# Row sums formed early, two groups in the seventh block, and the seventh split issued behind the third's, in a macaron FFN

## The chip, the cores and the metric

One core of a Trainium2 chip runs one launch of the whole layer. The time is the device time of that launch in microseconds (us), the median of several runs. The engines are TensorE (PE; its weight loads are PEld), VectorE (DVE), ScalarE (ACT), GpSimd (POOL) and SyncE (SP, which issues most transfers).

## The reference

One layer on x of 256 tokens by 2048 columns in float32:

```
x = x + 0.5 * swiglu(rms_norm(x, ffn1_norm), w_gate1, w_up1, w_down1)
h = rms_norm(x, mix_norm);  u, q, k, v = split(h @ w_in)
x = x + concat(rms_norm(s5_mixer(u)), rms_norm(stick_breaking(q, k, v))) @ w_out
x = x + 0.5 * swiglu(rms_norm(x, ffn2_norm), w_gate2, w_up2, w_down2)
x = x + rms_norm((p @ w_ple_proj) * sigmoid(rms_norm(x, ple_norm) @ w_ple_gate), ple_post_norm)

swiglu(h, w_gate, w_up, w_down) = (silu(h @ w_gate) * (h @ w_up)) @ w_down
```

D_MODEL is 2048 and D_FF 5632. The change concerns the two FFNs, above all gate and up of the first.

## The kernel before

**Tiles.** The 256 tokens are two halves t of 128 rows. The 5632 columns of gate and up are eleven blocks f of 512 columns (f = 0 to 10, the "first" to the "eleventh" block). The 2048 rows of a weight are 16 tiles of 128, taken in four quarters kb of four tiles: one load on SP's queue brings 128 x 4 x 512 floats (1 MB) into a `raw` tile, of which there are five buffers.

**Split numbers.** To get float32 accuracy from the fast matmul form each operand is the sum of a high and a low part. For a weight half (two of the four tiles, 128 x 1024) ACT casts the high part (`split`, L181: `whi` or `shi`) and DVE subtracts it from the original for the low part (L184: `wlo` or `slo`). Three products are formed, high x high, high x low of the activations, and low x high: in an ordinary half (`gemm_half`, L322, L323, L327) these are 12 matmuls of 128 x 128 x 512. `weight_pair` hands out the buffers from two rings that alternate, "whi"/"wlo" with four buffers and, in the blocks with seven products, "shi"/"slo" with three. So the letters w and s are buffers, not kinds of operands.

**Seven products for eight.** The class `Seven` (from L463) treats gate and up together. `column` is the ordinary way for one of the two matrices and some quarters. `chunk` (L505) does one quarter of both, a group, with seven products instead of eight. It loads two raw tiles, gate (halves b11, b21) and up (halves b12, b22); forms t1 = b11 + b12, t2 = t1 + b22 and t4 = t2 + b21 on DVE (L501); lets a transfer on POOL's queue add b22 into b12 in place (L525, an accumulating DMA); and issues the products in the order 1 (b11), 5 (t1), 6 (t2), 4 (t4), 2 (b21), 3 (b22), 7 (the b12 that the transfer has changed). Each product is one split and six matmuls (L494, L495, L497), 42 for a group where two ordinary quarters issue 48. On the side of the activations it needs sums of rows: `whole_rows` joins high and low (DVE, L443), `sum_forms` makes four sums (DVE, L458) and splits them (ACT, then DVE: `hhi`, `hlo`).

**The blocks.** In the first FFN the blocks f = 0 to 5 go the ordinary way, since the preparation of the S5 mixer (`s5_prep`, small DVE and ACT instructions, L765 and following) holds memory beside them; `early` is 6. At f = 6 the preparation is finished, its memory is given back, and the row sums of both groups are formed. This seventh block does one group, kb = 0, and takes the other three quarters of both matrices by `column`. The blocks f = 7 to 10 do two groups (kb = 0 and 1). In the second FFN all blocks use `Seven`, the first with one group. The down projections mix groups and columns by a plan.

**The order.** A scheduler gives each engine its order of instructions; the program's order is its starting point, and it may put an instruction ahead of earlier ones that aren't ready by its own reckoning. Each engine then works its queue strictly in order. `step()` advances work that stands beside the main loop, `put_off(n, fn)` calls fn after n such steps, and the positions of instructions can be tied with `pin` or with the scheduler's `issue_after`, under which what is issued in the block stands behind a given instruction. A pool opened with `phase` takes the memory that earlier pools have left, tile by tile.

Of the kernel before, what the change touches and what calls it, by code (L numbers as in the profile page):

```python
# [26 lines left out]
NB = 512  # L27
# [6 lines left out]
def layer_kernel(ctx: ExitStack, tc: tile.TileContext, a: dict, shapes: dict, out: bass.AP):  # L34
# [143 lines left out]
    def split(hi, lo, src, scale=None, pinned=False):  # L178

        if scale is None:  # L180
            copy = nc.scalar.copy(hi, src)  # L181
            if pinned:
                pin(copy)
            nc.vector.tensor_tensor(out=lo, in0=src, in1=hi.bitcast(F32), op=ALU.subtract)  # L184
        else:
            split_each(hi.unsqueeze(1), lo.unsqueeze(1), src.unsqueeze(1), [scale])
# [276 lines left out]
    class Seven:  # L463


        def __init__(self, act, sums, ws, pool):
            self.act, self.sums, self.ws, self.pool = act, sums, ws, pool
            self.banks = {}
            self.begun = set()
# [17 lines left out]
        def product(self, z, left, src, final):  # L487
            hi, lo = weight_pair()
            split(hi, lo, src)
            ps = self.bank(z)  # L490
# [13 lines left out]
        def chunk(self, kb, final=()):  # L504

            if ring[0] is None:
                ring[:] = [self.pool, 0]
            raws = []
# [12 lines left out]
            def summed(z):  # L521
                return [[u[:, z, j * P : (j + 1) * P] for j in range(2)] for u in sums]
# [11 lines left out]
            self.product(2, whole(1, 0), b21, final)  # L534
            self.product(3, summed(3), b22, final)
            step()
            self.product(7, summed(2), b12, final)
            step()
# [16 lines left out]
    def ffn(i, xn, nxt, bg=None):  # L555
# [3 lines left out]
        early = 6 if bg else 0  # L559
        sevens = None if bg else pools.enter_context(sums_phase(f"sums{i}"))  # L560
        hp = pools.enter_context(phase(f"h{i}"))
        side = ExitStack()
        prep = bg(side) if bg else None
        mids = {}

# [13 lines left out]
        for f in range(NF):  # L579
            if prep and f == early:  # L580
                finish(prep)
                side.close()
                prep = None
                sevens = pools.enter_context(sums_phase(f"sums{i}"))
                hp = pools.enter_context(phase(f"h{i}b"))
                sums = [sum_forms(sevens, whole_rows(sevens, xn(kb)), "h") for kb in range(2)]
            if sevens:
                sg, hh = com("sg"), com("h")
# [15 lines left out]

                s = Seven(xn, lambda kb: sums[kb], ((wg, f * NB), (wu, f * NB)), sevens)
                if f == 0:
                    sums = [sum_forms(sevens, whole_rows(sevens, xn(0)))]
                    s.column(0, (1,))
# [6 lines left out]
                    sums.append(sum_forms(sevens, whole_rows(sevens, xn(1))))  # L615
                elif f == early:
                    s.column(0, (1, 2, 3))
                    s.chunk(0, (*shared, 2, 4))
                    put_off(0, opened, s)
                else:  # L620
                    s.chunk(0)
                    s.column(0, (2, 3))
                    s.chunk(1, (*shared, 2, 4))
                    put_off(0, opened, s)
                put_off(0, gated, s)
                s.column(1, (3,) if f == 0 else (1, 2, 3) if f == early else (2, 3), True)
                nc.vector.tensor_tensor(out=hh, in0=s.banks[3.8], in1=hh, op=ALU.add)
# [4 lines left out]
                put_off(2, turned, hp, f, hh)  # L632
                continue

            def gate():
# [71 lines left out]
        for n in range(0, ND, 2):  # L707
# [6 lines left out]

            s = Seven(kept, summed, ((wd, n * NB), (wd, (n + 1) * NB)), sevens)
            plan = plans[n // 2]
# [965 lines left out]
```

## Time and profile before

| | us |
|---|---|
| median of three runs | 1828.03 |
| the three runs | 1827.74 to 1829.2 |
| the profiled execution, whole time | 1829.07 |
| its span, first to last instruction | 1827.3 |

The mean granted TensorE clock of the profiled execution is 0.998 of full speed. Weights make most of the 425 MB that are moved. A row of the timeline has the start in us from the span's begin, the duration in us, the engine, the line, the operation, what is written from what, the shape, how many instructions the row holds, and in brackets the idle time ahead of it and what ended that. A row of windows has the stretch, its length, the busy time of PE, PEld, DVE, ACT and POOL with their number of instructions, the granted clock, the share of the DMA engines and GB/s. A row of waits has the total, the number and the longest. Successive matmuls overlap in the records, so a rate is read from one start to the next.

### The profile page before, as it was taken

How to read it: one execution, taken by the hardware profiler on the slowest of the kernel's cores; microseconds unless marked ns; L12 is line 12 of the kernel's file. 1: busy time of each engine (PE TensorE's matmuls, PEld its weight loads, DVE VectorE, ACT ScalarE, POOL GpSimd, SP SyncE). 2: the span in 40 equal slices, each digit the busy share in tenths (PEclk: the TensorE clock that was granted, in tenths of full speed). 3: DMA queues.
4: the chain of work that ended last, by engine and by line, in shares of the span. 5: the costliest groups of instructions: out<-in, count | busy, mean ns of one | idle time of the engine just before them, and what ended most of it. 6: DMA issues, size and time to landing. Idle time of an engine off the chain costs nothing.

```text
span 1827.3 us, 24177 instructions
## 1 busy us (share of the span) xinstructions
PE 1817.7 (99%) x8954; PEld 1504.9 (82%) x8954; DVE 1518.4 (83%) x1773; ACT 1048.0 (57%) x1220; POOL 101.0 (6%) x156
## 2 busy tenths in 40 slices
PE   9999999999999999999999999999999999999998
PEld 7888888888888888888898888888878888888887
DVE  8966759999898885697567899999989999888565
ACT  7444445655565665456695566555555556556554
POOL 0010000000000001010021000000000010000000
PEclk9999999999999999999999999999999999999999
DMA  9899877787777677674646788887777787667563
GB/s 328 282 286 281 247 226 231 235 246 220 254 246 238 189 250 229 186 252 156 220 149 213 241 280 234 265 258 222 241 220 236 237 274 241 226 202 250 172 217 127
DMA packets 234407, 425.27 MB, mean 233 GB/s; under 512 B 24272, under 2 KB 48240, under 8 KB 234128
## 3 DMA queue, kind: packets, MB, share of 16 engines
q1 hardware_dynamic: 223872, 390.06, 64.9%
q0 software_dynamic: 9696, 32.25, 8.1%
q8 instruction: 70, 1.15, 0.3%
q10 hardware_dynamic: 720, 1.41, 0.2%
q14 instruction: 49, 0.40, 0.1%
HBM read 372.41 MB, written 10.88 MB: 210 GB/s over the span
## 4 chain that ended last, share of the span: by engine, by line
PE 98%; DMA 1%; DVE 0%; ACT 0%; issue 0%; SPq 0%; ACTq 0%; DVEq 0%
PE acc L322 18%; PE acc L323 18%; PE acc L327 18%; PE aux L323 7%; PE aux L327 7%; PE aux L322 7%; PE acc L497 4%; PE acc L495 4%; PE acc L494 4%; PE aux L497 3%; PE aux L495 3%; PE aux L494 3%; DMA raw<-raw 1%; PE aux L1142 0%; PE acc L1398 0%; PE acc L1393 0%
## 5 line engine op out<-in xcount | busy, mean ns | idle before, releaser
L184 DVE TENSOR_TENSOR wlo<-raw,whi 128x1024 fp32r<-128x1024 f32 x486 | 589.0, 1224 | 179.3 <-ACT whi L181 177.9
L181 ACT CAST whi<-raw 128x1024 fp32r<-128x1024 f32 x486 | 505.3, 1050 | 352.5 <-PE acc L323 234.7
L322 PE MATMUL acc<-whi,nhi 128*128 128x512 f32 x1052 | 412.4, 392 | 0.9 <-ACT whi L181 0.4
L323 PE MATMUL acc<-whi,nlo 128*128 128x512 f32 x1052 | 409.6, 389 | 0.0
L327 PE MATMUL acc<-wlo,nhi 128*128 128x512 f32 x1052 | 288.8, 389 | 0.0
L184 DVE TENSOR_TENSOR slo<-raw,shi 128x1024 fp32r<-128x1024 f32 x180 | 219.2, 1218 | 32.7 <-ACT shi L181 31.3
L322 PEld LDWEIGHTS acc<-whi,nhi 128*128 128x128 f32 x1052 | 197.6, 188 | 43.9 <-ACT whi L273 1.4
L181 ACT CAST shi<-raw 128x1024 fp32r<-128x1024 f32 x180 | 188.7, 1050 | 76.1 <-DMA raw<-in_ffn_w_down 22.8
L327 PEld LDWEIGHTS acc<-wlo,nhi 128*128 128x128 f32 x1052 | 197.5, 188 | 41.1
L323 PEld LDWEIGHTS acc<-whi,nlo 128*128 128x128 f32 x1052 | 197.6, 188 | 40.1
L181 ACT CAST whi<-sum 128x1024 fp32r<-128x1024 f32 x68 | 71.6, 1053 | 136.5 <-DVE sum L501 129.9
L181 ACT CAST shi<-sum 128x1024 fp32r<-128x1024 f32 x52 | 54.8, 1053 | 85.4 <-DVE sum L501 83.0
L501 DVE TENSOR_TENSOR sum<-sum,raw 128x1024 f32<-128x1024 f32 x80 | 97.6, 1220 | 0.7
L525 POOL DMA_DIRECT2D raw<-raw x40 | 34.7, 868 | 955.3 <-DVE sum L501 657.6
L184 DVE TENSOR_TENSOR wlo<-sum,whi 128x1024 fp32r<-128x1024 f32 x68 | 83.1, 1221 | 2.4 <-ACT whi L181 1.6
L184 DVE TENSOR_TENSOR slo<-sum,shi 128x1024 fp32r<-128x1024 f32 x52 | 63.5, 1221 | 2.4 <-ACT shi L181 1.9
L322 PE MATMUL aux<-whi,hhi 128*128 128x512 f32 x168 | 65.4, 389 | 0.0
L323 PE MATMUL aux<-whi,hlo 128*128 128x512 f32 x168 | 65.4, 389 | 0.0
L323 PE MATMUL acc<-whi,hlo 128*128 128x512 f32 x160 | 62.3, 390 | 0.0
L322 PE MATMUL acc<-whi,hhi 128*128 128x512 f32 x160 | 62.2, 389 | 0.0
L322 PE MATMUL aux<-whi,nhi 128*128 128x512 f32 x156 | 60.7, 389 | 0.0
L323 PE MATMUL aux<-whi,nlo 128*128 128x512 f32 x156 | 60.7, 389 | 0.0
(375 smaller groups left out, 3200.2 us busy)
## 6 DMA issues: line engine op xcount, KB each, us to landing
raw<-in_ffn_w_up SPq DMA_DIRECT2D x88, 1024.0 KB, 6.1
raw<-in_ffn_w_down SPq DMA_DIRECT2D x88, 1024.0 KB, 5.3
raw<-in_ffn_w_gate SPq DMA_DIRECT2D x86, 1024.0 KB, 8.0
raw<-in_w_in SPq DMA_DIRECT2D x32, 1024.0 KB, 5.8
raw<-raw POOLq DMA_DIRECT2D x40, 512.0 KB, 5.9
raw<-in_w_out SPq DMA_DIRECT2D x16, 1024.0 KB, 5.2
raw<-in_w_ple_gate SPq DMA_DIRECT2D x16, 1024.0 KB, 5.3
hT<-mid SPq DMA_DIRECT2D x160, 64.0 KB, 4.3
```

Of the source, the lines that this page charges most:

```text
L181: copy = nc.scalar.copy(hi, src)
L184: nc.vector.tensor_tensor(out=lo, in0=src, in1=hi.bitcast(F32), op=ALU.subtract)
L322: nc.tensor.matmul(ps[t], lhsT=lh, rhs=hi[:, j, cols], start=start and j == 0, stop=False)
L323: nc.tensor.matmul(ps[t], lhsT=ll, rhs=hi[:, j, cols], start=False, stop=False)
L327: nc.tensor.matmul(ps[t], lhsT=lh, rhs=lo[:, j, cols], start=False, stop=stop and j == 1)
L494: nc.tensor.matmul(ps, lhsT=lh[j], rhs=hi[:, j], start=begin and j == 0, stop=False)
L495: nc.tensor.matmul(ps, lhsT=ll[j], rhs=hi[:, j], start=False, stop=False)
L497: nc.tensor.matmul(ps, lhsT=lh[j], rhs=lo[:, j], start=False, stop=z in final and j == 1)
L501: nc.vector.tensor_tensor(out=t, in0=x, in1=y, op=ALU.add)
L525: nc.gpsimd.dma_start(b12, b22, accum_op=ALU.add)
```

## The change

`split` now returns its two instructions, and in every group of both FFNs, the down projections included, the split and the matmuls of product 7 are issued behind the cast and the subtraction of product 3. The row sums of the first FFN's two groups are no longer formed at the seventh block but put off from the start of the sixth (f = 5), by 8 and 12 steps. Their pool (`sevens`) opens at the start of the FFN; the "shi"/"slo" ring gets a pool of its own (`turns`) at the seventh block. That block takes the ordinary path of the blocks behind it: two groups, and the quarters 2 and 3 by `column`.

```diff
@@ split
-            nc.vector.tensor_tensor(out=lo, in0=src, in1=hi.bitcast(F32), op=ALU.subtract)
+            rest = nc.vector.tensor_tensor(out=lo, in0=src, in1=hi.bitcast(F32), op=ALU.subtract)
+            return copy.ins, rest.ins
@@ class Seven, product
-            split(hi, lo, src)
+            self.last = split(hi, lo, src)
@@ class Seven, chunk
             if ring[0] is None:
-                ring[:] = [self.pool, 0]
+                ring[:] = [self.turns, 0]
...
             self.product(3, summed(3), b22, final)
+            copied, rest = self.last
             step()
-            self.product(7, summed(2), b12, final)
+            with tc.issue_after(copied), tc.issue_after(rest):
+                self.product(7, summed(2), b12, final)
@@ ffn
         early = 6 if bg else 0
-        sevens = None if bg else pools.enter_context(sums_phase(f"sums{i}"))
+        sevens = pools.enter_context(sums_phase(f"sums{i}"))
...
+        turns = sevens
+        sums = []
...
                 side.close()
                 prep = None
-                sevens = pools.enter_context(sums_phase(f"sums{i}"))
+                turns = pools.enter_context(phase(f"turns{i}"))
                 hp = pools.enter_context(phase(f"h{i}b"))
-                sums = [sum_forms(sevens, whole_rows(sevens, xn(kb)), "h") for kb in range(2)]
-            if sevens:
+            if f >= early:
...
-                elif f == early:
-                    s.column(0, (1, 2, 3))
-                    s.chunk(0, (*shared, 2, 4))
-                    put_off(0, opened, s)
                 else:
                     s.chunk(0)
                     s.column(0, (2, 3))
                     s.chunk(1, (*shared, 2, 4))
                     put_off(0, opened, s)
                 put_off(0, gated, s)
-                s.column(1, (3,) if f == 0 else (1, 2, 3) if f == early else (2, 3), True)
+                s.column(1, (2, 3) if f else (3,), True)
...
+            if f == early - 1:
+                for kb in range(2):
+                    put_off(8 + 4 * kb, lambda kb: sums.append(sum_forms(sevens, whole_rows(sevens, xn(kb)), "h")), kb)
```

Lines behind these places stand one to four further down in the changed program (L184 stays, L443 becomes L444, L494 becomes L495).

First place: ACT's queue at the second group of the eighth block in the second FFN. A `raw` with the smaller number (11500, 11517) is gate, the one with the larger (11502, 11519) is up; `shi_11571` is the cast of the seventh product before, `whi_11561` that of the third, `whi_11541` that of the fourth.

```order
L181 CAST whi_11507<-raw_11500 128x1024
L181 CAST shi_11517<-sum_11504 128x1024
L181 CAST shi_11551<-raw_11500 128x1024
L181 CAST whi_11529<-sum_11527 128x1024
L181 CAST shi_11571<-raw_11502 128x1024
L181 CAST whi_11541<-sum_11539 128x1024
L181 CAST whi_11561<-raw_11502 128x1024
L181 CAST whi_11583<-raw_11581 128x1024
```

And in the changed program, where the seventh is `shi_11588`, the third `whi_11578` and the fourth `whi_11558`:

```order
L181 CAST whi_11524<-raw_11517 128x1024
L181 CAST shi_11534<-sum_11521 128x1024
L181 CAST shi_11568<-raw_11517 128x1024
L181 CAST whi_11546<-sum_11544 128x1024
L181 CAST whi_11558<-sum_11556 128x1024
L181 CAST whi_11578<-raw_11519 128x1024
L181 CAST shi_11588<-raw_11519 128x1024
L181 CAST whi_11600<-raw_11598 128x1024
```

The seventh's cast has moved behind the fourth's and the third's; the subtractions on DVE have moved in the same way. Of the 40 groups before, five have the seventh's cast ahead of the third's on ACT: that of the seventh block in the first FFN and four in the second FFN.

Second place: ACT's queue at the seventh block's group in the first FFN. Before, `whi_2708` is the seventh, `shi_2677` the fourth and `shi_2697` the third; the raw tiles 2718 belong to the column behind it.

```order
L181 CAST whi_2640<-raw_2633 128x1024
L181 CAST shi_2651<-sum_2637 128x1024
L181 CAST whi_2664<-sum_2662 128x1024
L181 CAST whi_2687<-raw_2633 128x1024
L181 CAST whi_2708<-raw_2635 128x1024
L181 CAST whi_2720<-raw_2718 128x1024
L181 CAST shi_2677<-sum_2675 128x1024
L181 CAST shi_2697<-raw_2635 128x1024
```

And in the changed program, at the first group of that block, with `shi_2573` the fourth, `shi_2595` the third and `whi_2609` the seventh:

```order
L181 CAST whi_2536<-raw_2529 128x1024
L181 CAST whi_2560<-sum_2558 128x1024
L181 CAST shi_2547<-sum_2533 128x1024
L181 CAST whi_2584<-raw_2529 128x1024
L181 CAST shi_2573<-sum_2571 128x1024
L181 CAST shi_2595<-raw_2531 128x1024
L181 CAST whi_2609<-raw_2531 128x1024
L181 CAST whi_2621<-raw_2619 128x1024
```

The seventh has moved from ahead of the fourth to behind the third, and the column's first cast behind all of them.

Third place: DVE's queue at the start of the program, in the first block's second quarter (`nlo` are the low parts of the activations). Before:

```order
L277 TENSOR_TENSOR wlo_147<-raw_132,whi_146 128x512
L193 SCALAR_TENSOR_TENSOR nlo_165<-h_138,gains,nhi_164 128x256 x4
L184 TENSOR_TENSOR wlo_201<-raw_133,whi_200 128x1024
L184 TENSOR_TENSOR wlo_205<-raw_133,whi_204 128x1024
L193 SCALAR_TENSOR_TENSOR nlo_223<-sg_220,gains,nhi_222 128x256 x4
```

And in the changed program:

```order
L278 TENSOR_TENSOR wlo_150<-raw_135,whi_149 128x512
L194 SCALAR_TENSOR_TENSOR nlo_168<-h_141,gains,nhi_167 128x256 x4
L444 TENSOR_TENSOR whole_2363<-nhi_145,nlo_146 128x1024
L184 TENSOR_TENSOR wlo_204<-raw_136,whi_203 128x1024
L184 TENSOR_TENSOR wlo_208<-raw_136,whi_207 128x1024
L194 SCALAR_TENSOR_TENSOR nlo_226<-sg_223,gains,nhi_225 128x256 x4
```

The first of the row sums' instructions (`whole`, the join of high and low) stands in the first block, ahead of the second quarter's first low half; the rest of both groups' row sums follow it in the same block, between the low halves and the instructions of the S5 preparation, which stand further back by that.

In all, TensorE issues six matmuls fewer, DVE six instructions more, ACT three more, and POOL one accumulating transfer more (41 instead of 40).

More of the change, by code (lines that the diff above doesn't have):

```diff
@@ L463, in layer_kernel, with __init__ @@
     class Seven:
-        def __init__(self, act, sums, ws, pool):
-            self.act, self.sums, self.ws, self.pool = act, sums, ws, pool
+        def __init__(self, act, sums, ws, pool, turns):
+            self.act, self.sums, self.ws, self.pool, self.turns = act, sums, ws, pool, turns
             self.banks = {}
@@ L603, in gated @@
                     )
-                s = Seven(xn, lambda kb: sums[kb], ((wg, f * NB), (wu, f * NB)), sevens)
+                s = Seven(xn, lambda kb: sums[kb], ((wg, f * NB), (wu, f * NB)), sevens, turns)
                 if f == 0:
-                    sums = [sum_forms(sevens, whole_rows(sevens, xn(0)))]
+                    sums.append(sum_forms(sevens, whole_rows(sevens, xn(0))))
                     s.column(0, (1,))
@@ L713, in end @@
                 put_off(0 if m == ND - 1 and m < nxt.early else 2, nxt.block, m)
-            s = Seven(kept, summed, ((wd, n * NB), (wd, (n + 1) * NB)), sevens)
+            s = Seven(kept, summed, ((wd, n * NB), (wd, (n + 1) * NB)), sevens, turns)
             plan = plans[n // 2]
```

## The prediction

> **What bounds the kernel now.** I read the page's first and fourth parts first, to see which engine sets the end.
>
> ```profile
> span 1827.3 us, 24177 instructions
> PE 1817.7 (99%) x8954; PEld 1504.9 (82%) x8954; DVE 1518.4 (83%) x1773; ACT 1048.0 (57%) x1220; POOL 101.0 (6%) x156
> PE 98%; DMA 1%; DVE 0%; ACT 0%; issue 0%; SPq 0%; ACTq 0%; DVEq 0%
> ```
>
> TensorE is busy 1817.7 of 1827.3 us and holds 98% of the chain that ended last. So only three things can move the time: the number of matmuls, the gaps between them, and the rate at which they run. How fast do they run undisturbed? The timeline of PE alone, in an easy stretch, has two heads of equal groups of six:
>
> ```profile
> 1328.70 0.39 PE L322 MATMUL acc<-whi,nhi 128*128 128x512 f32 x1
> 1330.06 0.39 PE L322 MATMUL acc<-whi,nhi 128*128 128x512 f32 x1
> ```
>
> 1330.06 - 1328.70 = 1.36 us for six, 0.227 each (the 0.39 of a row overlaps the next one). Next the waits of PE by what released them, which say where the gaps are:
>
> ```profile
> PE acc L494 <- ACT whi L181: 1.9, 1, 1.9
> PE acc L322 <- ACT whi L181: 0.4, 1, 0.4
> PE aux L497 <- DVE wlo L184: 0.4, 1, 0.4
> ```
>
> The columns are the total, the number of times and the longest. One wait, 1.9 us at L494, is most of it. The "DMA 1%" of the chain points at the same place, so I read the timeline and the chain there (the eighth block of the second FFN, its second group).
>
> ```profile
> 1333.96 9.53 DMA raw<-raw
> 1338.92 1.22 DVE L501 TENSOR_TENSOR sum<-sum,raw 128x1024 f32<-128x1024 f32 x1
> 1343.65 1.04 ACT L181 CAST shi<-raw 128x1024 fp32r<-128x1024 f32 x1 [6.97 <-DMA raw<-raw]
> 1344.60 1.04 ACT L181 CAST whi<-sum 128x1024 fp32r<-128x1024 f32 x1
> 1345.55 1.99 ACT L181 CAST whi<-raw 128x1024 fp32r<-128x1024 f32 x2
> 1344.73 1.23 DVE L184 TENSOR_TENSOR slo<-raw,shi 128x1024 fp32r<-128x1024 f32 x1 [4.59 <-ACT shi L181]
> 1345.87 1.22 DVE L184 TENSOR_TENSOR wlo<-sum,whi 128x1024 fp32r<-128x1024 f32 x1
> 1343.21 0.61 PE L497 MATMUL aux<-wlo,nhi 128*128 128x512 f32 x2
> 1345.70 0.50 PE L494 MATMUL acc<-whi,hhi 128*128 128x512 f32 x1 [1.87 <-ACT whi L181]
> 1347.14 1.22 PE L497 MATMUL acc<-wlo,hhi 128*128 128x512 f32 x2 [0.25 <-DVE wlo L184]
> 1350.65 0.39 PE L494 MATMUL aux<-whi,nhi 128*128 128x512 f32 x1
> 1345.60:1348.00 2.40, 2.06 (x6) 1.44 (x7) 2.40 (x3) 2.40 (x4) 0.00 (x0) 0.82 0.04 15
> 1348.00:1350.60 2.60, 2.60 (x7) 2.04 (x7) 2.60 (x4) 2.60 (x4) 0.00 (x0) 0.51 0.37 62
> ```
>
> This is a queue standing behind a transfer. The accumulating DMA, which makes the seventh product's weights in place (b12 += b22), takes 9.53 us and lands at 1343.49. ACT has the seventh's cast (1343.65) ahead of the fourth's (1344.60) and the third's, and idles 6.97 us, though the fourth's sum has been ready since 1338.92 + 1.22 = 1340.14. PE, whose order is 4, 2, 3, 7, waits for the fourth's cast. The last two rows are windows; the eighth column, behind POOL's, is the granted TensorE clock: it falls to 0.82 and then 0.51, so the wait is paid twice.
>
> What is lost there: product 6's last matmul begins one pitch behind 1343.21, at 1343.44, so the fourth would begin at 1343.67 and the third two products later, at 1343.67 + 2 x 1.36 = 1346.39. It begins at 1350.65: **4.26 us lost**, 2.03 of it the late begin (1345.70 - 1343.67), the other 2.23 in twelve matmuls that take 4.95 instead of 2.72, mostly the half clock.
>
> [...]
>
> **The change part by part.**
>
> *Seven behind three.* The two forced positions hold ACT's cast and DVE's low half of product 7 until those of product 3 are issued. In the order of the changed program this moves something in five of the 40 groups: the seventh block of the first FFN, and four groups of the second, of which the one above is the only one that PE waits at. There ACT would cast the fourth from 1340.14 and the third after it, both done by about 1340.14 + 2 x 1.05 = 1342.24, ahead of PE. The seventh, cast at 1343.65 with its low half ended at 1345.96, is needed by PE from 1343.67 + 3 x 1.36 = 1347.75 on, its low half at 1348.66: 2.7 us to spare. So -4.26.
>
> What is late next? DVE did both low halves behind the seventh's; now it does them in the 4.59 us it idled, and comes out two splits, 2.27 us (2 x 1.14, its pitch 1344.73 to 1345.87), earlier, whereas PE comes out 4.26 earlier. DVE's lead over PE shrinks by 1.99.
>
> ```profile
> 1370.44 1.18 DVE L184 TENSOR_TENSOR wlo<-raw,whi 128x1024 fp32r<-128x1024 f32 x1
> 1373.35 0.62 PE L497 MATMUL aux<-wlo,nhi 128*128 128x512 f32 x2
> 1350.70:1391.00 40.30, 40.30 (x179) 33.36 (x178) 40.09 (x39) 24.05 (x26) 1.72 (x2) 1.00 0.79 233
> 1394.40 0.69 DVE L593 TENSOR_TENSOR h<-aux,sg 128x512 f32<-128x512 f32 x1 [2.12 <-PE aux L497]
> ```
>
> The smallest lead behind it is at this low half, ended 1371.62 and used at 1373.35: 1.73. So PE would wait 1.99 - 1.73 = 0.26 there: **+0.3** given back. The window's DVE column (40.09 of 40.30) says that DVE can't catch up by itself, and the last row that at 1394.40 it waits 2.12 us for PE, which renews the lead. That renewal is what holds the give-back at 0.3; without it the whole 1.99 is lost at later places with smaller leads, as this one, where PE already waits:
>
> ```profile
> 1083.26 0.73 PE L497 MATMUL aux<-wlo,nhi 128*128 128x512 f32 x2 [0.40 <-DVE wlo L184]
> ```
>
> *Two groups in the seventh block.* A group through seven products issues 42 matmuls where two ordinary columns issue 48; one more group is converted, so six matmuls go: 6 x 0.227 = **-1.36**. DVE's part must stay below PE's, and it does: the block gains six splits and sums (28 instead of 22, 6 x 1.14 = 6.8 us) and loses the row sums (8.2 us, below), 1.4 less in all, as PE has 1.36 less; the two-group blocks behind it have the new mix already.
>
> *The seventh block's own small stall* goes with the old order, in which the seventh's cast stood ahead of the fourth's:
>
> ```profile
> 292.87 0.61 PE L497 MATMUL aux<-wlo,hhi 128*128 128x512 f32 x2
> 293.44 0.50 PE L494 MATMUL acc<-shi,nhi 128*128 128x512 f32 x1
> 294.71 0.74 PE L497 MATMUL acc<-slo,nhi 128*128 128x512 f32 x2
> 295.28 0.40 PE L494 MATMUL acc<-whi,nhi 128*128 128x512 f32 x1
> 293.43 1.23 DVE L184 TENSOR_TENSOR slo<-sum,shi 128x1024 fp32r<-128x1024 f32 x1 [0.58 <-ACT shi L181]
> ```
>
> From 292.87 to 295.28 there are eight matmuls, 2.41 us against 8 x 0.23 = 1.84: **-0.57**.
>
> *The row sums.* They are written into the sixth block, but in the changed program's order they stand far ahead of it, in the first block, since all that they need is there by then. DVE's first of them comes between the second quarter's activations and its first low half:
>
> ```profile
> 10.76 1.67 DVE L193 SCALAR_TENSOR_TENSOR nlo<-h,gains,nhi 128x256 fp32r<-128x256 f32 x4
> 12.63 2.36 DVE L184 TENSOR_TENSOR wlo<-raw,whi 128x1024 fp32r<-128x1024 f32 x2 [0.19 <-ACT whi L181]
> 14.59 1.07 PE L327 MATMUL acc<-wlo,nhi 128*128 128x512 f32 x4
> L443 DVE TENSOR_TENSOR whole<-nhi,nlo x2: 1218/1222/1226, 269.0 to 272.9; 128x1024 f32<-128x1024 f32 x2
> L458 DVE TENSOR_TENSOR rows<-whole x8: 418/418/425, 270.3 to 1062.3; 128x256 f32<-128x256 f32 x8
> ```
>
> The low half that PE needs at 14.59 ended at 12.63 + 1.22 = 13.85. Put 1.22 ahead of it (or 1.14, the pitch), less the 0.19 that DVE idled there, and it ends at 14.80 to 14.88: **+0.3**, with the half clock not counted for so short a gap. Bounds: 0 if it starts earlier than I think; 0.74 lead lost entirely plus 1.2, i.e. 1.2, if the ACT side slips too. The rest, 8.2 us of DVE in all (twice 1.22 + 4 x 0.42 + 1.22), pushes the S5 preparation back instead of the low halves. I counted in the changed order how much more DVE work stands ahead of each low half: at most 7.6 us, at about 100 us:
>
> ```profile
> 99.69 1.23 DVE L184 TENSOR_TENSOR wlo<-raw,whi 128x1024 fp32r<-128x1024 f32 x1 [1.32 <-ACT whi L181]
> 107.33 1.07 PE L327 MATMUL acc<-wlo,nhi 128*128 128x512 f32 x4
> 91.40:110.00 18.60, 18.60 (x83) 15.40 (x83) 15.12 (x21) 7.49 (x9) 4.21 (x9) 1.00 1.00 272
> ```
>
> This low half ends at 100.92 and is used at 107.33, a lead of 6.41; but DVE idles 18.60 - 15.12 = 3.48 in this window, 1.32 of it right here. 7.6 - 6.41 = 1.2 is the most that PE could wait, and the idleness covers it: 0, with 1.2 as the upper bound.
>
> *The sum* on the profiled execution, whose whole time is 1829.07: -4.26 + 0.3 - 1.36 - 0.57 + 0.3 = -5.6, so 1823.5. That execution is the slowest but one of those shown (median 1828.03); the same terms from the median give 1822.4. The truth lies between, as the half clock may be milder in the runs that aren't profiled: **1823.0 us**.
>
> **The rivals.** A measurement of this kernel can tell about 0.2% from no change, 3.7 us: below 1824.4 is faster, above 1831.7 slower.
>
> *The lead isn't renewed* (15%). Behind 1345 DVE stays 1.99 behind, and PE gives that back wherever DVE is the last to end. For it: DVE has 40.09 of 40.30, and the renewal hangs on the one row at 1394.40. Against it: that wait of 2.12 exceeds 1.99. It gives 1823.0 + 1.7 = 1824.7; within 0.2%.
>
> *The stall is in the profiled execution alone* (9%). The seventh's DMA takes 4.5 to 9.5 us over the 40 groups, as this row of L525 has it (minimum, median, maximum), and this was the longest:
>
> ```profile
> DMA to landing us min/median/max: 4.5/5.9/9.5
> ```
>
> With a landing below 1340.1 nothing is lost, and then only the other terms are left: 1828.03 - 1.36 - 0.57 + 0.3 = 1826.4, within 0.2%. Against it: the three runs are within 1.46 us of one another and of the profiled one, where this would make 4.26 of difference.
>
> *The change doesn't do what it says* (8%): row sums stand in the first block and cost more there than they save. With the bounds 1.2 at the start and 1.2 at 100 us in place of 0.3 and 0, the time is 1823.0 + 2.1 = 1825.1.
>
> *Slower* (13%): the first block's DVE queue. If the 8.2 us of row sums delay the low halves by their full length, because the S5 steps pushed back have their own waits for ACT and these hold DVE up in turn, PE loses up to 8.2, and 2.2 more to one spell of half clock as at 1348: 1823.0 + 8.2 + 2.2 = 1833.4. It decides from the point at which DVE has no idle time left between 12 and 110 us. For it: DVE is busy at once from 10.76 on and the first lead is 0.74. Against it: the lead has grown to 6.41 by 100 us, and DVE idled 3.48 of the last 18.60 us.
>
> **How the numbers follow.** The forecast has 55%. Its own range is 1821.5 to 1824.4 (all bounds of small terms in their good or bad sense). Faster: 55 and the better half of the third rival, some 5, 60%. Within 0.2%: 15 + 9 + 3 = 27%. Slower: 13%. The range 1821.3 to 1828.0 holds the first four cases nearly whole and leaves out the slower one and some 6% below.
>
> **What would show it.** No gap on PE longer than half a microsecond around the eighth block of the second FFN, ACT's casts there in the order fourth, third, seventh, and a granted clock of 1.00 in that window: right on the first step. A PE wait of under 0.4 us some 28 us behind it and none of a microsecond later: right on the give-back. PE with 8948 matmuls or so, six fewer: the third term. DVE's whole sum standing at 12 us, and PE's first low-half matmul of the second quarter at about 14.9: the cost of the start. The prediction is wrong if a new wait of over a microsecond on PE shows up anywhere between 12 and 300 us, or if another seventh cast, behind its third, holds ACT while PE waits for a cast behind it.

## The result

| | us |
|---|---|
| before, median of 9 runs | 1827.56 (1825.54 to 1829.20) |
| changed, median of 9 runs | 1823.35 (1822.71 to 1824.01) |
| changed, profiled execution | 1823.55, span 1821.8 |

The ratio is 0.9976 with a 95% interval of 0.9968 to 0.9984: 4.2 us faster, and the runs lie closer together. The two profiled spans differ by 1827.3 - 1821.8 = 5.5 us.

The changed kernel's page, first part, and the waits of its PE (total, number, longest):

```profile
span 1821.8 us, 24173 instructions
PE 1814.3 (100%) x8948; PEld 1503.3 (83%) x8948; DVE 1523.6 (84%) x1779; ACT 1048.4 (58%) x1223; POOL 102.6 (6%) x157
...
PE aux L249 <- POOL ones L125: 1.1, 1, 1.1
PE aux L324 <- DVE hlo L184: 0.4, 1, 0.4
PE acc L323 <- ACT whi L181: 0.4, 1, 0.4
PE aux L498 <- DVE wlo L184: 0.2, 1, 0.2
```

The 1.9 us at the fourth product (L494 before, L495 now) is gone; six matmuls are gone (8954 to 8948); the wait at 1083 us, behind the low half, has fallen from 0.4 to 0.2; one at `hlo` is new. The timeline of ACT and PE, with two windows, at the second group of the eighth block in the second FFN:

```profile
1339.31 1.05 ACT L181 CAST whi<-sum 128x1024 fp32r<-128x1024 f32 x1 [3.49 <-DVE sum L502]
1340.26 1.05 ACT L181 CAST whi<-raw 128x1024 fp32r<-128x1024 f32 x1
1341.22 1.05 ACT L181 CAST shi<-raw 128x1024 fp32r<-128x1024 f32 x1
...
1342.34 0.61 PE L498 MATMUL aux<-wlo,nhi 128*128 128x512 f32 x2
1342.79 0.39 PE L495 MATMUL acc<-whi,hhi 128*128 128x512 f32 x1
1345.51 0.39 PE L495 MATMUL aux<-whi,nhi 128*128 128x512 f32 x1
1346.87 0.39 PE L495 MATMUL aux<-shi,nhi 128*128 128x512 f32 x1
...
1341.00:1344.00 3.00, 3.00 (x15) 2.49 (x14) 3.00 (x4) 3.00 (x4) 0.00 (x0) 1.00 0.88 324
1344.00:1347.00 3.00, 3.00 (x15) 2.49 (x14) 3.00 (x3) 3.00 (x5) 0.00 (x0) 1.00 0.63 160
```

ACT casts the fourth, the third and then the seventh. The fourth product begins one pitch behind the sixth's last matmul (1342.34 + 2 x 0.227 = 1342.79), the third and the seventh follow without a gap, PE is busy for every microsecond, and the clock is 1.00.

To see where the rest went, I compared the start of the same matmul in both profiles, counted from the last one back. The difference of the changed profile against before grows along the program so (us):

| stretch | difference in it | what it is |
|---|---|---|
| first matmul to 36 | +0.48 | the start |
| one group more | -1.36 | six matmuls |
| 36 to 270 | -0.16 | small differences |
| seventh block, to 316 | -0.60 | its stall |
| 316 to 686 | -0.10 | small differences |
| 686 to 720 | +0.73 | hand-over to the mixer |
| mixer, to 1035 | +0.42 | small waits |
| 1083 | -0.25 | DVE's low half |
| 1341 to 1355 | -4.30 | the stall at the fourth product |
| to the end | -0.41 | small waits |
| sum | -5.55 | |

### The profile page after: what moved, and what is told of

Same layout as the page of the kernel before. It is cut to its first block, busy times and chain, and to the rows that moved or that the text cites. A ratio compares the mean times of both kernels' runs of the same rounds, so it can differ in the third digit from the quotient of the medians.

```text
span 1821.8 us, 24173 instructions
## 1 busy us (share of the span) xinstructions
PE 1814.3 (100%) x8948; PEld 1503.3 (83%) x8948; DVE 1523.6 (84%) x1779; ACT 1048.4 (58%) x1223; POOL 102.6 (6%) x157
## 4 chain that ended last, share of the span: by engine, by line
PE 95%; SPq 1%; DMA 1%; ACT 1%; DVE 1%; issue 0%; ACTq 0%; DVEq 0%
PE acc L323 17%; PE acc L324 17%; PE acc L328 17%; PE aux L324 6%; PE aux L328 6%; PE aux L323 6%; PE acc L498 4%; PE acc L496 4%; PE acc L495 4%; PE aux L498 3%; PE aux L496 3%; PE aux L495 3%; SPq L1192 1%; DMA raw<-in_w_in 1%; SPq L230 1%; PE aux L1146 0%
## 5 line engine op out<-in xcount | busy, mean ns | idle before, releaser
L184 DVE TENSOR_TENSOR wlo<-raw,whi 128x1024 fp32r<-128x1024 f32 x485 | 587.8, 1224 | 172.2 <-ACT whi L181 171.3
L323 PE MATMUL acc<-whi,nhi 128*128 128x512 f32 x1036 | 406.7, 393 | 0.7 <-ACT whi L181 0.4
L324 PE MATMUL acc<-whi,nlo 128*128 128x512 f32 x1036 | 403.7, 390 | 0.0
L328 PE MATMUL acc<-wlo,nhi 128*128 128x512 f32 x1036 | 284.0, 389 | 0.0
L184 DVE TENSOR_TENSOR slo<-raw,shi 128x1024 fp32r<-128x1024 f32 x181 | 220.1, 1216 | 21.4 <-ACT shi L181 20.1
L323 PEld LDWEIGHTS acc<-whi,nhi 128*128 128x128 f32 x1036 | 194.8, 188 | 43.4 <-ACT whi L181 1.4
L184 DVE TENSOR_TENSOR wlo<-sum,whi 128x1024 fp32r<-128x1024 f32 x68 | 83.0, 1220 | 3.8 <-ACT whi L181 3.1
L184 DVE TENSOR_TENSOR slo<-sum,shi 128x1024 fp32r<-128x1024 f32 x55 | 67.1, 1220 | 1.0 <-ACT shi L181 0.5
L323 PE MATMUL aux<-whi,hhi 128*128 128x512 f32 x164 | 63.8, 389 | 0.0
L323 PE MATMUL acc<-whi,hhi 128*128 128x512 f32 x164 | 63.8, 389 | 0.0
L323 PE MATMUL aux<-whi,nhi 128*128 128x512 f32 x152 | 59.1, 389 | 0.0
```

The costliest lines, as they stand in the source:

```text
L184: rest = nc.vector.tensor_tensor(out=lo, in0=src, in1=hi.bitcast(F32), op=ALU.subtract)
L323: nc.tensor.matmul(ps[t], lhsT=lh, rhs=hi[:, j, cols], start=start and j == 0, stop=False)
L324: nc.tensor.matmul(ps[t], lhsT=ll, rhs=hi[:, j, cols], start=False, stop=False)
L328: nc.tensor.matmul(ps[t], lhsT=lh, rhs=lo[:, j, cols], start=False, stop=stop and j == 1)
```

## The experiments

**The order alone** (before, with the seventh behind the third's in all groups):

```diff
+            copied, rest = self.last
             step()
-            self.product(7, summed(2), b12, final)
+            with tc.issue_after(copied), tc.issue_after(rest):
+                self.product(7, summed(2), b12, final)
```

> The seventh split behind the third's in every group, nothing else; the row sums and the single group of the seventh block stay as before. Theory (the gain is the cast that stood ahead of the fourth's, behind the transfer): the 1.87 us wait at the eighth block of the second FFN and the half clock behind it are gone, the 0.57 us in the seventh block of the first FFN too, so about 3.5 us below before (1824), that is four fifths of what the change gave. Rival (that wait is large in the profiled execution alone): 0.6 us below before, 1827. Rival (the gain comes from the early sums and the second group): no difference from before.

Measured: 1823.94 against 1827.26 of before on the same chip (ratio 0.9983, 0.9975 to 0.9992), 3.3 below. PE has no wait at the fourth product and none in the seventh block of the first FFN. So the order holds four fifths of the gain, and the wait was no feature of one execution.

**The early sums and the second group alone** (the change, with the order left to the scheduler, which has the seventh ahead in five groups again):

```diff
-            with tc.issue_after(copied), tc.issue_after(rest):
-                self.product(7, summed(2), b12, final)
+            self.product(7, summed(2), b12, final)
```

> The row sums early and two groups in the seventh block, with the split of the seventh product left in the scheduler's order, which has it ahead of the third's in the same five places as before. Theory: six matmuls off (-1.36 us), the start 0.4 us later, the waits in the eighth block of the second FFN as before, so about 0.9 below before (1826.7), and PE's wait of about 2 us behind the cast in the eighth block in its profile. Rival (the gain comes from the early sums and the second group): the whole 4.2, 1823.4. Rival (that wait comes and goes with the transfer's chance): no PE wait of over 0.5 us at that place.

Measured: 1824.64 against 1827.26 (0.9987, 0.9978 to 0.9996), 2.6 below where 0.9 was expected: a miss. The wait at the fourth product was there, but smaller; the runs spread from 1823.55 to 1828.20. PE's rows there, and the window behind:

```profile
1344.13 0.50 PE L495 MATMUL acc<-whi,hhi 128*128 128x512 f32 x1 [0.55 <-ACT whi L181]
1345.59 0.73 PE L498 MATMUL acc<-wlo,hhi 128*128 128x512 f32 x2 [0.25 <-DVE wlo L184]
...
1346.00:1348.60 2.60, 2.60 (x13) 2.17 (x12) 2.60 (x3) 2.60 (x4) 0.00 (x0) 1.00 0.34 48
```

The transfer landed 8.16 us after its issue instead of 9.53, the wait is 0.55 instead of 1.87, and the clock stays at 1.00. A second, new wait of 0.44 us stands at 1322.79, in the group ahead of it. The two halves of the change give 3.3 and 2.6 alone and 4.2 together, so they overlap by about 1.7, of which the seventh block's 0.6 is removed by either. Why the wait was smaller in this profile is taken up below. The second wait has the same cause: the accumulating transfer of that group took 6.51 us (4.73 in the profile of before), ACT has the seventh's cast ahead of the fourth's there too, and PE loses 0.8 us.

```profile
1320.74 1.05 ACT L181 CAST whi<-raw 128x1024 fp32r<-128x1024 f32 x1 [3.94 <-DMA raw<-raw]
1322.79 0.50 PE L495 MATMUL acc<-shi,hhi 128*128 128x512 f32 x1 [0.44 <-ACT shi L181]
```

**One group in order** (before; only the second group of the second FFN's eighth block):

```diff
+            with ExitStack() as behind:
+                if self.held == kb:
+                    behind.enter_context(tc.issue_after(copied))
+                    behind.enter_context(tc.issue_after(rest))
+                self.product(7, summed(2), b12, final)
...
+                s.held = 1 if i == 2 and f == 7 else None
```

> As before, with the seventh behind the third's in a single group out of 40, the second one of the second FFN's eighth block. Theory: this group holds nearly all of the gain of the order: 3 to 4 us below before (1824), 0.6 short of the order in all groups, which is the seventh block of the first FFN. Rival (the other four places matter as much in runs that aren't profiled): less than half of what the order in all groups gives.

Measured: 1825.00 against 1827.26 (0.9986, 0.9977 to 0.9995), 2.3 below; 1.1 short of all groups in order, where 0.6 had been expected for the seventh block. By the medians this group holds two thirds of the order's gain, less than the 3 to 4 us expected from a profile that lost 4.26 there.

**The other groups in order** (the complement, `self.held != kb`):

> As before, with the seventh behind the third's in every group but that one, the complement of the one group in order. Theory: PE's wait in the eighth block of the second FFN stays, between 1 and 4.3 us by the landing; the other four places give 0.6 us in the seventh block of the first FFN and nothing elsewhere, so 0.6 to 1.0 below before (1826.5). Rival (the four other places hold as much as that group in the runs that aren't profiled): 2 us or more below before.

Measured: 1826.23 against 1828.02 (0.9989, 0.9980 to 0.9998), 1.8 below, more than the 0.6 to 1.0 expected and short of the rival's 2; the interval, 0.4 to 3.7 us, takes in both. Its profile shows the wait in the one group left as it was; the seventh block's is gone. The rival has a part of the truth. In the third profile of before (below) PE also loses 0.5 us at 1242 us, in another of the four groups (its matmuls start 0.1 behind those of the first profile up to there, and 0.6 behind them two microseconds on), where the transfer took 6.18 us instead of the first profile's 4.52. ACT and PE there, and PE's row in the first profile:

```profile
1239.97 1.05 ACT L181 CAST whi<-raw 128x1024 fp32r<-128x1024 f32 x1 [3.60 <-DMA raw<-raw]
1242.02 0.50 PE L494 MATMUL acc<-shi,hhi 128*128 128x512 f32 x1
...
1241.63 0.39 PE L494 MATMUL acc<-shi,hhi 128*128 128x512 f32 x1
```

It loses 0.4 more at 1324 us, behind a transfer of 6.05. So the four other places hold more than the seventh block's 0.6 in some executions; how much on the average isn't measured.

**The transfer left out in that group** (order as before; the seventh product there uses b12 alone):

```diff
-            nc.gpsimd.dma_start(b12, b22, accum_op=ALU.add)
+            if self.marked != kb:
+                nc.gpsimd.dma_start(b12, b22, accum_op=ALU.add)
```

> As before in every queue's order, with the accumulating transfer left out in one group, the second of the second FFN's eighth block (its seventh product then uses b12 alone). Theory (the cast is late because it waits for the transfer's landing): PE's wait at the fourth product is gone although the seventh's cast still stands ahead of it; the time is that of the one group put in order, 2.3 us below before (1825.0). Rival (it is the order of casts on a full ACT that makes the fourth late): PE still waits there, and the time is that of before, 1827.3.

Measured: 1824.88 against 1828.02 (0.9983, 0.9974 to 0.9991), 3.1 below. ACT's timeline:

```profile
1339.89 1.05 ACT L181 CAST shi<-raw 128x1024 fp32r<-128x1024 f32 x1 [2.69 <-PE acc L323]
1340.84 1.05 ACT L181 CAST whi<-sum 128x1024 fp32r<-128x1024 f32 x1
```

The seventh's cast still stands ahead of the fourth's, but waits no longer for a DMA (by the row it waits for PE's L323), and PE loses nothing there. It was the transfer's landing, through ACT's queue, that held the fourth.

**The transfer done twice in that group, under the new order** (the seventh product there uses b12 + 2 b22):

```diff
-            nc.gpsimd.dma_start(b12, b22, accum_op=ALU.add)
+            for _ in range(2 if self.marked == kb else 1):
+                nc.gpsimd.dma_start(b12, b22, accum_op=ALU.add)
```

> The change, with the accumulating transfer of that same group done twice, one behind the other (its seventh product then uses b12 + 2 b22). Theory: in the change's profile the transfer lands at 1341.13 and the seventh's cast is needed from about 1345.8 on, 4.7 us of cover; a second transfer takes 4.5 to 9.5 us by the profiles, so PE loses 0 to 5 us there, about 2.5 (1826), and all of it at the seventh product, none at the fourth. Rival (the order has no cover of its own, it only fell on earlier landings): the whole second transfer is lost, 5 us or more, from the fourth product on (1829 or more).

Measured: 1828.46, the time of before on the same chip (1828.02; 1.0005, 0.9996 to 1.0014), so the whole gain of the change is gone: some 4.6 us by the medians, 4.9 in the profile, twice the 2.5 expected and near the rival's size. The place is the theory's: ACT, PE and DVE of this kernel:

```profile
1339.34 1.05 ACT L181 CAST whi<-raw 128x1024 fp32r<-128x1024 f32 x1
1346.46 1.04 ACT L181 CAST shi<-raw 128x1024 fp32r<-128x1024 f32 x1 [6.08 <-DMA raw<-raw]
...
1345.49 0.61 PE L499 MATMUL aux<-wlo,nhi 128*128 128x512 f32 x2
1347.56 0.50 PE L496 MATMUL aux<-shi,nhi 128*128 128x512 f32 x1 [1.46 <-ACT shi L181]
1348.82 0.72 PE L499 MATMUL aux<-slo,nhi 128*128 128x512 f32 x2
1367.25 0.74 PE L499 MATMUL acc<-wlo,hhi 128*128 128x512 f32 x2 [1.57 <-DVE wlo L184]
...
1347.54 1.23 DVE L184 TENSOR_TENSOR slo<-raw,shi 128x1024 fp32r<-128x1024 f32 x1 [5.71 <-ACT shi L181]
1365.98 1.22 DVE L184 TENSOR_TENSOR wlo<-sum,whi 128x1024 fp32r<-128x1024 f32 x1
```

The fourth, second and third products run on time, and PE waits first at the seventh, due at 1345.49 + 2 x 0.227 = 1345.94 and begun at 1347.56. With the low half's delay, 2.1 us are lost there by the starts of the same matmuls. The seventh's cast begins 1.10 ahead of the product (1347.56 - 1346.46), so for the product's begin it could have begun as late as 1344.84, 2.98 behind the fourth product's begin (1341.86 here). The low half allows less: it is used 2.36 behind the cast's begin (1348.82 - 1346.46) and was due at 1345.94 + 4 x 0.227 = 1346.85, so the cast could begin at no cost until 1344.49, 2.63 behind the fourth's begin. In the change it begins 1.57 ahead of that (1341.22 and 1342.79). The cover is the sum, 4.2 us; 4.7 had been worked out. But DVE has the seventh's low half at the head of its queue too, and idles 5.71 us behind it. Its lead is used up, and 20 us later PE waits for its low halves, 1.57 at 1367.25 and 0.37 at 1372.03, and 2.8 us more are lost. Theory and rival each had one half: the order covers the late landing for ACT and PE, not for DVE.

**The row sums held back** (the change, with the row sums kept behind the sixth block's own splits):

```diff
+                def formed(kb):
+                    copied, rest = newest
+                    with tc.issue_after(copied), tc.issue_after(rest):
+                        sums.append(sum_forms(sevens, whole_rows(sevens, xn(kb)), "h"))
```

(`newest` is the last ordinary split.)

> The change with the row sums held behind the sixth block's own splits, where they were written, instead of in the first block. Theory: the join of high and low leaves the second quarter's first low half at the start alone, and PE begins these matmuls 0.3 us earlier; the sixth block's DVE has room. So 0.3 us below the change (1823.0). Rival (early row sums are what lets the seventh block run, or DVE's room at the sixth block is short): 0.5 us or more above the change, with a PE wait in the sixth or seventh block.

Measured: 1822.97 against 1827.26 (0.9975, 0.9966 to 0.9984). Against the change the difference of 0.4 in median is within the spread of runs, but the profiles show where it is. DVE and PE at the start of the change:

```profile
12.53 1.22 DVE L444 TENSOR_TENSOR whole<-nhi,nlo 128x1024 f32<-128x1024 f32 x1
13.67 2.35 DVE L184 TENSOR_TENSOR wlo<-raw,whi 128x1024 fp32r<-128x1024 f32 x2
...
14.54 0.39 PE L324 MATMUL acc<-whi,nlo 128*128 128x512 f32 x1
14.94 1.20 PE L328 MATMUL acc<-wlo,nhi 128*128 128x512 f32 x4
```

and DVE with the sums held back:

```profile
10.76 1.67 DVE L194 SCALAR_TENSOR_TENSOR nlo<-h,gains,nhi 128x256 fp32r<-128x256 f32 x4
12.63 2.36 DVE L184 TENSOR_TENSOR wlo<-raw,whi 128x1024 fp32r<-128x1024 f32 x2 [0.20 <-ACT whi L181]
```

The low half is back at 12.63, and PE's matmul of index 600 is 0.46 earlier than in the change, 0.17 of which the start of both programs differs by anyway. PE has no wait in the sixth or seventh block: the sixth has the room.

**The transposes later too** (the kernel above, with the second FFN's first block turned six steps behind it instead of two):

```diff
-                put_off(2, turned, hp, f, hh)
+                put_off(6 if f == 0 else 2, turned, hp, f, hh)
```

> The row sums held to the sixth block, and the two transposes behind the second FFN's first block put off by six steps instead of two, so that they stand behind the low half that PE waits for at 1083 us. Theory: PE's wait of 0.2 to 0.6 there goes, DVE's work is the same and only later; 0.4 below the row sums held late alone (1822.6). Rival (DVE has no room behind it either): the wait appears 35 us further back, where the lead is 0.5, and the time is that of the row sums held late, 1823.0.

Measured: 1822.41 against 1828.02 (0.9969, 0.9958 to 0.9981). The rival's later wait doesn't appear; PE's waits in this kernel are all at the start and the end:

```profile
PE aux L249 <- POOL ones L125: 1.1, 1, 1.1
PE acc L325 <- ACT whi L274: 0.5, 1, 0.5
PE acc L325 <- ACT whi L181: 0.4, 1, 0.4
PE aux L1598 <- ACT diag L1597: 0.2, 1, 0.2
```

Between the matmuls at 1044 and 1147 this profile gains 0.71 us on the one with the sums held back alone, of which 0.41 is the wait behind the transposes. But that wait comes and goes: it is missing too in the profiles of the other groups in order and of the sums and second group alone, which leave the transposes where they were. This kernel's median is 0.9 below the change's, but the two were measured on different chips.

**The change and this kernel once more, side by side on one chip:**

> The change itself, beside the next kernel on one chip. Theory: 1823.4, as measured first, with no wait at the fourth product of the second FFN's eighth block whatever the landing of the transfer there. Rival (its gain hung on an early landing): 2 us more, with a wait in that group.

> The row sums held to the sixth block and the first block's transposes put off, a second time and on the same chip as the change. Theory: 0.3 for the start and 0.2 to 0.6 for the wait at 1083 us, so 0.5 to 1.0 below the change. Rival (the difference seen before was one of chips): within 0.3 of the change.

Measured: the change 1822.81 against 1827.06 (0.9976, 0.9966 to 0.9986), the kernel with both later 1822.70 (0.9974, 0.9964 to 0.9985). The change's gain stands, and PE waits nowhere in the one group although the transfer took 8.29 us (nor does it with the order alone, where it took 9.09). The further step isn't shown to gain: 0.1 us, the rival's case. By the profiles the 0.29 at the start is there, and 0.3 between 1079 and 1147; the change's own wait at 1083 was small this time, and other waits, in the mixer and near the end, differ by more than that from one execution to the next.

**Before, twice more**, for the size of the wait:

> The kernel before, profiled once more. Theory (the first profile had a spell of half clock that most executions don't have): the transfer takes 8 to 9.5 us again, PE waits 0.5 to 2 us at the fourth product, and with a wait below about 1.6 us the clock stays at 1.00 behind it, so the loss there is 1.4 to 2.5 us instead of 4.3 and the profiled time some 2 us below the first's 1829.07. Rival (the spell belongs to this place in every execution): a clock near 0.5 behind the wait again.

> The kernel before, a third profile, with the same two readings: by the theory the loss at the fourth product follows the landing of the transfer, one microsecond for one, and the half clock comes only with the longest waits; by the rival the half clock is there whatever the wait.

Profiled times of 1828.40 and 1827.87, 0.7 and 1.2 below the first's 1829.07, where some 2 had been expected. With the other two kernels that keep the old order in this group, five profiles show the wait (us; "due" is one pitch behind the sixth product's last matmul, "late" the fourth's begin after it, "lost" counted to the third's begin):

| kernel | transfer, issue to landing | landing - due | late | granted clock behind | lost |
|---|---|---|---|---|---|
| before, first | 9.53 | -0.17 | 2.03 | 0.53 | 4.26 |
| before, second | 9.23 | -0.49 | 1.71 | 0.53 | 3.97 |
| before, third | 8.70 | -0.97 | 1.22 | 1.00 | 1.93 |
| other groups in order | 9.19 | -0.49 | 1.70 | 1.00 | 2.37 |
| sums and second group alone | 8.16 | -1.49 | 0.71 | 1.00 | 1.37 |

In every row "late" is "landing - due" + 2.20: the landing's microsecond is PE's microsecond, behind the 2.20 of the seventh's cast and the fourth's. To this come 0.66 to 0.71 for the low half, which DVE does behind the seventh's. The windows of the second profile of before, of the third, and of the kernel with the other groups in order, from the first microseconds behind the wait on:

```profile
1347.00:1349.00 2.00, 1.95 (x5) 1.56 (x6) 2.00 (x2) 2.00 (x4) 0.00 (x0) 0.53 0.00 0
```

```profile
1347.00:1349.00 2.00, 1.74 (x8) 1.36 (x8) 2.00 (x3) 2.00 (x3) 0.00 (x0) 1.00 0.00 0
```

```profile
1345.00:1347.00 2.00, 1.75 (x9) 1.10 (x8) 2.00 (x3) 2.00 (x4) 0.00 (x0) 1.00 0.00 0
```

Clock 0.53, 1.00 and 1.00. The theory's first half holds (one for one with the landing). Its second half, full clock behind a wait below about 1.6 us, doesn't: a wait of 1.55 was followed by half clock in the second profile of before, one of 1.54 by full clock in the kernel with the other groups in order. Nor does the rival's: the clock doesn't fall each time.

What separates the cases can be read from the times at which the clock changes. In the first profile of before the trace has full clock granted from 5.69 to 1347.13 us, half clock to 1350.55 and full clock to 1825.00: 393, 1 and 139 times 3.4133 us. In the changed kernel's it has full clock from 7.12 to 1819.60, 531 times that. So I laid stretches of this length on each span, counted from a change of the clock. In windows on these stretches, for the second profile of before and for the other groups in order, the clock stands behind POOL's column and PE's busy time in front:

```profile
1343.69:1347.11 3.42, 1.63 (x7) 0.73 (x5) 2.48 (x3) 3.42 (x4) 0.00 (x0) 1.00 0.39 149
1347.11:1350.52 3.41, 3.41 (x8) 2.73 (x9) 3.41 (x4) 3.41 (x5) 0.00 (x0) 0.50 0.31 58
...
1339.64:1343.05 3.41, 3.10 (x14) 2.24 (x12) 0.00 (x0) 0.81 (x1) 0.00 (x0) 1.00 0.84 275
1343.05:1346.46 3.41, 1.93 (x7) 1.32 (x8) 3.15 (x3) 3.41 (x5) 0.00 (x0) 1.00 0.12 46
1346.46:1349.87 3.41, 3.41 (x16) 2.82 (x16) 3.41 (x4) 3.41 (x5) 0.00 (x0) 1.00 0.53 154
```

In the first of the two, the wait and the 0.24 us at the low half fall into one stretch, 1.79 us of idleness (3.42 - 1.63), and the next stretch has half clock. In the other the same idleness falls into two stretches, 0.31 and 1.48, and the clock stays at 1.00. The first profile of before has 2.11 in one stretch, and 0.50 behind it; the stretch in which PE's work ends has 2.53, and 0.50 behind it; the others ahead of that have 0.40 at the most, from 5.69 on, and full clock behind them. The changed kernel's has 2.68 in the stretch in which PE's work ends, and 0.50 behind it, and ahead of that 0.43 at the most, from 7.12 on, with full clock. The third profile of before has 0.92 at the most around this wait. Over all fourteen profiles, from the first full clock on and with the end of PE's work included, each stretch with 1.79 us of idleness or more is followed by half clock, and none with 1.70 or less is.

## Why the prediction was right

1823.0 was forecast, 1823.35 measured, and the difference of the profiled spans was 5.5 where the sum had 5.6. Some of this closeness is luck. The forecast stood 5.0 below the median known then, 1828.03; the gain was 4.2, and before itself came out at 1827.56. And the five terms, as the two profiles have them, come to -5.95; small waits that no term had gave 0.4 back. By its steps:

*What bounds the kernel, and the stall.* The row "1343.65 ... 6.97 <-DMA raw<-raw" was read as a cast that waits for a transfer while the next cast in the queue could go. Leaving out the transfer and leaving the order, or the other way round, each removes PE's wait, so the reading is shown. The term of -4.26 came out as -4.30 between the two profiles; as the 4.26 was read from the same profile of before, this says that nothing is lost there any more, and not that most executions lost so much. That this group is the only one of the four that PE waits at holds for that profile alone: with transfers of 6.05 to 6.51 us PE lost 0.4 to 0.8 in two others.

*Its size in the runs that aren't profiled.* This was the one choice in the number, between 1823.5 from the profiled time and 1822.4 from the median, on the ground that half clock may be milder elsewhere. Three profiles of before lost 4.26, 3.97 and 1.93. So the loss varies by more than two microseconds, by the landing and by whether half clock follows, and the choice of a number between the two was right in kind; that the 33 runs of before on one chip spread from 1825.15 to 1830.73, and the order alone from 1823.21 to 1824.59, fits it. The first profile, 1829.07 and 1.5 above the median, was at the upper end of this; so its sum of -5.6 stands beside a measured -4.2. Half clock came after waits of 1.87 and 1.55 us, 2.11 and 1.79 of idleness in a stretch of 3.41. Behind one of 1.54 us, whose idleness fell into two stretches as 0.31 and 1.48, the clock stayed at 1.00.

*The lead given back, +0.3.* It came out as 0. The seventh's low half, the low half behind the transposes, and the use of the latter:

```profile
1342.67 1.22 DVE L184 TENSOR_TENSOR slo<-raw,shi 128x1024 fp32r<-128x1024 f32 x1
1365.92 1.19 DVE L184 TENSOR_TENSOR wlo<-raw,whi 128x1024 fp32r<-128x1024 f32 x1
...
1368.17 0.61 PE L498 MATMUL aux<-wlo,nhi 128*128 128x512 f32 x2
```

The lead is 1368.17 - 1367.11 = 1.06; it was 1.73, so it shrank by 0.67 and not by 1.99. The transfer landed after 8.02 us instead of 9.53, and DVE took up the seventh's low half at 1342.67. Landed after 9.53, at 1342.64, it would have held that low half until about 1343.88 (an estimate: in before the low half began 1.24 behind the landing, 1344.73 and 1343.49), 1.2 later, and the lead would have shrunk by nearly the whole 1.99. The mechanism itself is real: with the transfer done twice it cost 2.8 us at just this place.

*Six matmuls, -1.36, and the seventh block's stall, -0.57*: -1.36 and -0.60.

*The row sums, +0.3 at the start and 0 at 100 us.* The join pushes the low half's end to 13.67 + 1.22 = 14.89 and PE's use to 14.94; +0.48 at the start, 0.17 of which stands ahead of the join already, leaves 0.31. At 100 us nothing shows: the differences are the same from 36 to 104 us.

*What it didn't see.* The 0.73 at the hand-over to the mixer in that profile. By 686 us the changed kernel is 1.74 ahead, but ACT's activations wait for columns that come back by transfer, and these land only 0.5 us earlier, so PE waits at 699.75. ACT's row in the change:

```profile
696.59 0.91 ACT L192 ACTIVATE nhi<-h,gains 128x256 fp32r<-128x256 f32 x2 [5.02 <-DMA h<-mid]
```

and before:

```profile
697.10 0.91 ACT L191 ACTIVATE nhi<-h,gains 128x256 fp32r<-128x256 f32 x2 [3.79 <-DMA h<-mid]
```

In the change's second profile this wait is missing (between the same matmuls it is 0.70 us shorter), and it is missing too in the four profiles of the change with something added, so it looks like a matter of that transfer's chance and no part of the change.

The slower rival, row sums that delay the first block's low halves one after another, didn't happen: the low halves that DVE made between 85 and 110 us kept leads of 4.4 us or more, where they had 6.4 before. Of the other rivals, the stall in the profiled execution alone fell: all five profiles with the old order in that group have it. Whether a lost lead is renewed wasn't put to the test, as the lead never ran out in the change.

**Open.** Why the sums and the second group alone gave 2.6 and not the 0.9 expected, or 1.5 with the seventh block's 0.6. The shorter wait in its one profile fits (1.37 lost and not 2 to 4), but the transfer's length varies from 7.7 to 9.5 us over all profiles of this group, and one profile can't tell a shift of its mean from chance. That the order's five places don't add up exactly (2.3 and 1.8 apart, 3.3 together) is within the intervals. And that half clock goes with the idleness in one stretch, there with 1.79 us and not with 1.70, is read from waits that came about by themselves; no run varied the idleness alone.

## What to carry to other kernels

In a queue that is worked strictly in order, look for an instruction that waits for a transfer while what PE needs next is ready behind it; the row to look for is a long idle time "<-DMA" on an engine that isn't the bottleneck (here 6.97 us of ACT), followed by a short wait of PE "<-" that engine (1.87). Put the instruction in PE's order of need, and then ask how late the transfer may land, and which other engine has the same transfer's next step at the head of its queue: that engine's lead is the next to go, as DVE's did here, with 2.8 us of PE's time, when the transfer was done twice. Size the term from several executions: the wait on this landing was 1.87, 1.55 and 1.06 us in three of the same kernel.

## What the runs showed of the hardware

The same accumulating transfer of 512 KB in the same group took 7.7 to 9.5 us from issue to landing over the profiles, with the neighbours before and behind it at 4.5 to 6.5 and 7.5 to 8.4. A PE wait of 1.55 us was followed by 3.41 us at a granted clock of 0.50, whereas one of 1.54 wasn't, nor one of 1.57 with the transfer done twice (1.00). By the third product's begin 3.97 us were lost with the wait of 1.55 and 2.37 with that of 1.54, 1.6 less. In these profiles it is the idleness within one of the stretches of 3.413 us that goes with it: 1.79 us and more with half clock behind, 1.70 and less without.
